# A two-block network on one Trainium2 core: where the norms between two layers are issued, and a tile order that goes k by k

## The chip, the cores and the metric

One Trainium2 chip, one of its cores. The metric is the time of the whole program on the device in microseconds (us), as the median of a few runs. Every time below is from these runs or from one execution that the hardware profiler recorded.

## What is computed

Two blocks of two layers each work on 512 tokens (T) of width 1024 (D). A layer is a mixer (block 1: sparse attention and an mLSTM; block 2: sparse and stick-breaking attention) and a feed-forward part (ffn). Around every one of these eight parts stands the same frame:

```python
h = rms_norm(x, pre_gain) * scale + shift      # what the part reads
y = part(h)                                    # ends in a product with an output matrix
x = x + gate * rms_norm(y, post_gain)          # what the next frame reads
```

rms_norm divides a token's 1024 values by the root of their mean square. So between the last product of one part and the first product of the next there lie two norms over the whole width, one behind the other. There are eight such ends: seven boundaries between parts, and the end of the program.

## The kernel before

**Layout.** Activations stand with the width on the 128 partitions: eight tiles (KT = 8) of 128 x 512 for x, for y and for h. All large products are made of 128x128 weight blocks. fp32 accuracy comes from three fast products: a weight chunk and h are each split into a high and a low part, and `mm3` (lines 310 to 315) issues high x high, high x low and low x high, one behind the other, so a weight chunk of 1024 columns times 256 tokens is 8 x 3 = 24 matmuls.

**Weights.** `load` (line 257) brings a chunk by DMA from the SP queue into a `raw` buffer (RAW = 4), rounds it on ScalarE into `hi` (line 265) and subtracts on VectorE, or on GpSimd where `lo_eng` says so, into `lo` (line 267). There are HL = 4 buffers for `hi` and 4 for `lo`; one is free again when the last matmul that reads it is done. Block 1's mixer converts `lo` on GpSimd; the other parts use VectorE.

**Halves.** At a boundary the work is done in two halves of 256 tokens (HALVES). `out_proj` (line 493, end of a mixer) and `down2` (line 1074, end of an ffn) run their last NO = 7 or ND = 5 output tiles in `in_halves` (line 340): all of them on half 0, then in reverse order on half 1. While half 1 is multiplied, half 0 is finished: `post_norm` of half 0 (line 475) is issued at the start of half 1, `pre_norm` of half 0 (line 437) before the tile number LA = 2 (out_proj, 24 matmuls a tile) or LB = 1 (down2, 33 matmuls a tile) of half 1. Behind the last tile `end()` issues `post_norm` of half 1.

**What a norm is.** `post_norm` makes two matmuls with a matrix of ones (ssy, sql; each is two records in the trace), Ln and Exp on ScalarE (rstd), and for each of the eight tiles two operations on VectorE (yn line 488, x line 489). `pre_norm` squares the eight x on ScalarE (line 444), adds them in pairs on VectorE (line 446), makes four matmuls with ones (eight records), again Ln and Exp, and for each tile xn on VectorE (line 458), hh on ScalarE (line 460 or 462) and hl on VectorE (line 468 or 473); hl follows three tiles behind xn (LAG = 3).

**The first products of the next part.** `fm_split` (line 376) takes them: six chunks of an ffn (EARLY = 6), three of block 1's mixer, four of block 2's. It too runs `in_halves`: tile by tile on half 0, then in reverse on half 1. `norms` leaves `pre_norm` of half 1 in `self.pending`; `fm_split` issues it before tile LC = 4 of half 0 (ffn), or before tile LD = 2 (mixers). In a mixer four steps of a product with tokens on the partitions (`more`, 24 matmuls a step; steps 0 and 1 read half 0, steps 2 and 3 half 1) come at the start of half 1. KF = 3 or KM = 1 weight chunks are kept for half 1.

**Around it.** At the start of a mixer `spill` (line 519) writes the eight x to DRAM with eight DMAs from the SP queue. Ahead of layer 1's ffn in block 1, `rope_tables` (line 544) computes sine and cosine tables for block 2; it is called between `out_proj` and `ffn`. The program's order is a priority and not the order itself: a scheduler fills each engine's queue when the program is built, by its own estimate of when an operand is ready, so a ready matmul may be put ahead of an earlier one that is not. Once built, each engine takes its queue in order.

Of the kernel before, what the change touches and what calls it, by code (L numbers as in the profile page):

```python
# [18 lines left out]
P = 128  # L19
T = 512  # L20
D = 1024
KT = D // P
# [10 lines left out]
PS1 = 0  # L33
PS2 = 0
# [9 lines left out]
PH2 = 0  # L44
PXM = 0
SA = 0
LA = 2
LAG = 3
LOA = 40
NO = 7  # L50
LB = 1
LC = 4
LD = 2
WIN = 0
KF = 3
KM = 1
# [20 lines left out]
HALVES = (slice(0, 256), slice(256, 512))  # L77
# [31 lines left out]
def steps(it, n):  # L109
    for _ in range(n):  # L110
        next(it, None)
        yield


def seq(*parts):
    for p in parts:
        yield from p
# [5 lines left out]
def dbg(g):  # L123
    while g.gi_yieldfrom is not None and hasattr(g.gi_yieldfrom, "gi_code") and g.gi_code.co_name in ("seq",):
        g = g.gi_yieldfrom
    l = g.gi_frame.f_locals if g.gi_frame else {}
    NET[0].mark(g.gi_code.co_name + "".join(str(l[v]) for v in ("g", "t", "bi", "pr", "hd") if v in l and isinstance(l[v], int)))


def run(steps):  # L130

    while True:
        try:
            dbg(steps)
            next(steps)
        except StopIteration as e:
            return e.value
# [16 lines left out]
class Task:  # L154
# [3 lines left out]
    def __init__(self, gen, n, start, end, after=None):  # L158
        self.gen, self.n, self.start, self.end, self.after = gen, n, start, end, after or {}
        self.i, self.done = 0, False  # L160
# [26 lines left out]
class Net:  # L187
    def __init__(self, ctx, tc, A, out):
        self.ctx, self.tc, self.nc, self.A, self.out = ctx, tc, tc.nc, A, out
        self.uid = 0  # L190
        self.fence = None
        self.back = iter(())
        NET[:] = [self]
        self.ahead = 90
        self.lo_eng = None
        self.T1, self.T2 = T1, T2
        self.pe = []
        self.xd = None
        self.pending = lambda: None
        self.tables, self.users = None, []  # L200
        nc = self.nc
        pool = lambda name, **kw: ctx.enter_context(tc.tile_pool(name=name, bufs=1, **kw))
        self.cp = pool("const")
        self.wp = pool("weights")
        self.up = ctx.enter_context(tc.tile_pool(name="units", bufs=1, reuse_waits="tile"))
        self.sp = pool("small")
        self.pp = pool("psum", space=PSUM)
        self.dp = pool("dram", space=DRAM)

        self.ident = self.cp.tile([P, P], F32, name="ident")  # L210
        make_identity(nc, self.ident)
        self.ones = self.cp.tile([P, P], F32, name="ones")
        nc.vector.memset(self.ones, 1.0)
        self.ones_r = self.cp.tile([P, P], F32R, name="ones_r")
        nc.scalar.activation(self.ones_r, self.ones, AF.Copy)
        self.eps = self.cp.tile([P, 1], F32, name="eps")
        nc.vector.memset(self.eps, EPS)


        self.cmask = self.cp.tile([P, T], F32, name="cmask")  # L220
        nc.gpsimd.memset(self.cmask, 0.0)
        nc.gpsimd.affine_select(self.cmask[:, 384:], self.cmask[:, 384:], [[-1, P]], ALU.is_ge, -NEG,
                                base=0, channel_multiplier=1)

        self.tri = self.cp.tile([P, P], F32, name="tri")
        nc.gpsimd.memset(self.tri, 0.0)
        nc.gpsimd.affine_select(self.tri, self.tri, [[-1, P]], ALU.is_ge, NEG, base=0, channel_multiplier=1)
        self.x = [self.unit("x") for _ in range(KT)]
        for k in range(KT):
            nc.sync.dma_start(self.x[k], A["xT"][:, k, :])  # L230
# [131 lines left out]
    def norms(self, y, sqs, g, nxt, late):  # L362


        if nxt is None:
            steps = [lambda i=i: self.post_norm(HALVES[i], y, sqs, g, True) for i in range(2)]
            return {0: steps[0]}, steps[1], (None, None)
        h = self.new_h()
        post = [lambda i=i: self.post_norm(HALVES[i], y, sqs, g) for i in range(2)]
        pre = [lambda i=i: self.pre_norm(HALVES[i], *nxt, *h) for i in range(2)]  # L370
        self.pending = pre[1]
        if late == 0:
            return {0: lambda: (post[0](), pre[0]())}, post[1], h
        return {0: post[0], late: pre[0]}, post[1], h

    def fm_split(self, chunks, act, pool, more=None):

        tiles = [self.ps("pj" if i < PJ else "ps") for i, _ in enumerate(chunks)]  # L380

        begin = {LC if more is None else LD: self.pending}
        middle = {} if more is None else {0: lambda: run(steps(more, 4))}
        self.in_halves([(i, [src]) for i, src in enumerate(chunks)], KF if more is None else KM,
                       lambda i, ws, hs, _: self.fm(tiles[i], ws[0], 0, act, hs, range(KT)), pool,
                       begin, middle)
        return tiles

    def fm_fed(self, chunks, toks, n, act, feed):
# [103 lines left out]
    def out_proj(self, chunks, act, y, g, nxt, pool):  # L493
# [19 lines left out]
        self.unspill()  # L513
        middle, end, h = self.norms(y, (ss, last), g, nxt, LA)
        self.in_halves([(f, [src for _, src in chunks(f)]) for f in range(KT - ntail, KT)], KO, one, pool, {}, middle)
# [164 lines left out]
    def mix1(self, l, h, nxt, feed=None):  # L680
        nc, A, tc = self.nc, self.A, self.tc
        par = self.par[l]
        W = A["w1_in"][l]
        act = self.acc(*h)
        pc = lambda name, i=0: par[:, B1[name] + i:B1[name] + i + 1]
        self.lo_eng = nc.gpsimd if LO1 else None
        self.spill()
        self.mark("1.split")


# [9 lines left out]
        def ev_vm(i, t, ps):  # L700
            nc.scalar.activation(vm[t][:, i * 256:i * 256 + 256], ps, AF.Copy)

        def ev_va(i, t, ps):
# [4 lines left out]
                              lambda t, ps, i=i: ev_vm(i, t, ps[:, :256])) for i in range(2)]  # L708
        if feed is None:
            more = seq(*vms)  # L710
            pss = self.fm_split([W[0], W[1], W[2]], act, PS1, more)
            run(more)
        else:
            pss, tps = self.fm_fed([W[0], W[1], W[2]], [(range(4), W[23]), (range(4, 8), W[24])], 256, act, feed)
            for t in range(NB):
                ev_vm(0, t, tps[t])
            self.rope_tables(A["positions"])
            run(vms[1])
# [201 lines left out]
        more = [Task(self.modulation(0, (2, 3, 4)), 24, *w("md"))] if l == 0 else []  # L920
# [153 lines left out]
    def down2(self, chunks, act, y, g, nxt, pool):  # L1074
# [16 lines left out]
        self.use(LN_EXP)  # L1091
        middle, end, h = self.norms(lambda k, cs: y[k][:, cs], (ss, last), g, nxt, LB)
        self.in_halves([(f, [src for _, src in chunks(f)]) for f in range(KT - ntail, KT)], KD, one, pool, {}, middle)
# [55 lines left out]
    def mix2(self, l, h, nxt):  # L1149
        nc, A, tc = self.nc, self.A, self.tc  # L1150
        par = self.par2[l]
        W = A["w2_in"][l]
        act = self.acc(*h)
        pc = lambda name, i=0, n=1: par[:, B2[name] + i:B2[name] + i + n]
        self.spill()
        self.mark("2.split")
        if LO2: self.lo_eng = nc.gpsimd

        vsb = self.values_tiles()
        sb_values = self.values_steps(vsb, [(W[16 + 2 * i], W[17 + 2 * i]) for i in range(2)], act)  # L1160
        pss = self.fm_split([W[i] for i in range(4)], act, PS2, sb_values)
        a1, a2 = self.rope(pss[0], pss[1])
        c1, c2 = self.rope(pss[2], pss[3], 64)

# [172 lines left out]
        for i, it in enumerate(items):  # L1337
            g, t, bi = it
            n = (2, 4, 8, 8)[t]
# [396 lines left out]
```

## Time and profile before

| | |
|---|---|
| median of 3 runs | 3232.23 us (3228.86 to 3241.45) |
| the profiled execution | 3238.15 us, span 3236.2 us, mean granted TensorE clock 0.975 |
| TensorE matmul (PE) busy | 3060.6 us, 95% of the span, 16196 instructions |
| VectorE (DVE), ScalarE (ACT), GpSimd (POOL) busy | 1958.9, 1552.1, 338.4 us |
| chain that ended last | PE 69%, DVE 10%, issue 10%, ACT 5%, DMA 3%, POOL 2% |

The profile page gives, for each engine, the time in which it had an instruction running, the wait ahead of an instruction and what ended it, and the clock that TensorE was granted (1.00 is 2.4 GHz, 0.50 is 1.2 GHz). A matmul's recorded duration is longer than its distance to the next, since they are pipelined; so the pace is read from starts, or from the number of matmuls in a stretch.

### The profile page before, as it was taken

Reading aid. Unit: us, or ns where it says so; the run is one execution under the profiler, and the core shown is the slowest. Engines: PE = TensorE matmul, PEld = TensorE weight load, DVE = VectorE, ACT = ScalarE, POOL = GpSimd, SP = SyncE. Lnnn points to the kernel's source line nnn. Section 1 sums busy time; section 2 is a strip of 40 time slices with the busy share of each in tenths; the row PEclk is TensorE's granted clock in tenths of the full one; section 3 lists DMA queues with packets and bytes.
Section 4 is the critical chain, followed back from the end, with each engine's and each line's share of the span. In section 5 each row is a group of like instructions: output and inputs, shape, how many; then the busy total and the mean of one; then the engine's idle time right before and its main releaser. Section 6 shows DMA issues by size and latency. Waiting matters only on the chain.

```text
span 3236.2 us, 42643 instructions
## 1 busy us (share of the span) xinstructions
PE 3060.6 (95%) x16196; PEld 2552.1 (79%) x16196; DVE 1958.9 (61%) x3542; ACT 1552.1 (48%) x2768; POOL 338.4 (10%) x329
## 2 busy tenths in 40 slices
PE   6898899998999899999999998999989999999998
PEld 5674787887875688888988778888888878788887
DVE  6778575546477463235677676645566766676365
ACT  4445642234444652224477665534445866454343
POOL 4352000001442000000100111000002001200000
PEclk8899999998998999999999999999999999999999
DMA  7235365644322232323421123323243112332323
GB/s 229 82 109 197 99 215 188 214 130 149 102 89 78 72 114 83 112 86 112 150 76 40 57 68 133 115 91 104 85 158 115 40 46 72 111 118 84 112 86 107
DMA packets 118925, 358.40 MB, mean 111 GB/s; under 512 B 15408, under 2 KB 28464, under 8 KB 118720
## 3 DMA queue, kind: packets, MB, share of 16 engines
q1 hardware_dynamic: 118720, 355.68, 34.2%
q8 instruction: 127, 2.08, 0.3%
q14 instruction: 78, 0.64, 0.1%
HBM read 336.19 MB, written 8.42 MB: 106 GB/s over the span
## 4 chain that ended last, share of the span: by engine, by line
PE 69%; DVE 10%; issue 10%; ACT 5%; DMA 3%; POOL 2%; SPq 0%; POOLq 0%; DVEq 0%; ACTq 0%
PE ps L305 26%; PE op L305 12%; PE pj L305 11%; PE dn L305 7%; PE tk L305 4%; PE nrm L305 2%; PE po L305 2%; DMA wm<-in_w_mod_dram 2%; DVE wlo L267 1%; DVE yn L488 1%; PE pt L308 1%; DVE x L489 1%; POOL mg L1357 1%; ACT whi L265 1%; DVE wm L633 1%
## 5 line engine op out<-in xcount | busy, mean ns | idle before, releaser
L265 ACT ACTIVATE whi<-raw 128x1024 fp32r<-128x1024 f32 (+1 forms) x562 | 550.0, 980 | 812.1 <-PE ps L305 204.0
L267 DVE TENSOR_TENSOR wlo<-raw,whi 128x1024 fp32r<-128x1024 f32 x500 | 559.1, 1122 | 530.5 <-ACT whi L265 527.4
L305 PE MATMUL ps<-hh,whi 128*128 128x512 f32 (+1 forms) x1560 | 574.4, 368 | 0.0
L305 PE MATMUL ps<-hl,whi 128*128 128x512 f32 (+1 forms) x1560 | 572.9, 367 | 0.0
L305 PE MATMUL ps<-hh,wlo 128*128 128x512 f32 (+1 forms) x1560 | 572.7, 367 | 0.0
L305 PE MATMUL pj<-hh,whi 128*128 128x512 f32 (+1 forms) x944 | 357.0, 379 | 23.5 <-ACT hh L654 13.3
L305 PE MATMUL pj<-hl,whi 128*128 128x512 f32 (+1 forms) x944 | 354.2, 375 | 4.4 <-POOL hl L656 4.4
L305 PE MATMUL pj<-hh,wlo 128*128 128x512 f32 (+1 forms) x944 | 352.1, 373 | 0.0
L305 PEld LDWEIGHTS ps<-hh,whi 128*128 128x128 f32 x1560 | 295.4, 189 | 48.1
L305 PEld LDWEIGHTS ps<-hh,wlo 128*128 128x128 f32 x1560 | 295.2, 189 | 48.3
L305 PEld LDWEIGHTS ps<-hl,whi 128*128 128x128 f32 x1560 | 295.5, 189 | 47.9
L305 PEld LDWEIGHTS pj<-hh,whi 128*128 128x128 f32 x944 | 181.5, 193 | 65.9 <-ACT hh L654 15.7
L305 PEld LDWEIGHTS pj<-hl,whi 128*128 128x128 f32 x944 | 181.9, 193 | 35.4 <-POOL hl L656 6.6
L305 PEld LDWEIGHTS pj<-hh,wlo 128*128 128x128 f32 x944 | 181.6, 192 | 30.2 <-issue 1.0
L633 DVE CUSTOM_DVE_ANT_0 wm<-wm,cact 128x1024 f32<-128x1024 f32 x96 | 121.6, 1270 | 112.1 <-DMA wm<-in_w_mod_dram 110.2
L267 POOL TENSOR_TENSOR wlo<-raw,whi 128x1024 fp32r<-128x1024 f32 x62 | 153.5, 2491 | 285.3 <-ACT whi L265 180.2
L305 PE MATMUL op<-hidh,whi 128*128 128x256 f32 (+1 forms) x572 | 178.9, 313 | 0.0
L305 PE MATMUL op<-hidh,wlo 128*128 128x256 f32 (+1 forms) x572 | 177.4, 310 | 0.3 <-DVE wlo L267 0.3
L305 PE MATMUL op<-hidl,whi 128*128 128x256 f32 (+1 forms) x572 | 176.9, 309 | 0.0
L575 POOL TENSOR_TENSOR rp<-rp,rp 128x512 f32<-128x512 f32 (+1 forms) x20 | 28.7, 1437 | 1091.7 <-DVE rp L574 1002.5
L305 PE MATMUL dn<-hidh,whi 128*128 128x512 f32 x352 | 137.8, 391 | 2.3 <-ACT hidh L254 2.3
L305 PE MATMUL dn<-hidl,whi 128*128 128x512 f32 x352 | 137.6, 391 | 0.2 <-DVE hidl L255 0.2
(352 smaller groups left out, 6151.4 us busy)
## 6 DMA issues: line engine op xcount, KB each, us to landing
raw<-in_w_in_dram SPq DMA_DIRECT2D x134, 512.0 KB, 3.4
raw<-in_w_up_dram SPq DMA_DIRECT2D x100, 512.0 KB, 3.5
wm<-in_w_mod_dram SPq DMA_DIRECT2D x96, 512.0 KB, 4.4
raw<-in_w_gu_dram SPq DMA_DIRECT2D x94, 512.0 KB, 3.4
raw<-in_w_dn_dram SPq DMA_DIRECT2D x80, 512.0 KB, 3.5
raw<-in_w_out_dram SPq DMA_DIRECT2D x52, 512.0 KB, 3.5
raw<-in_w_dn_dram SPq DMA_DIRECT2D x80, 192.0 KB, 3.1
hp<-rp SPq DMA_DIRECT2D x96, 64.0 KB, 2.0
```

Source lines behind the costliest of these rows:

```text
L265: nc_.scalar.activation(hi[:, :n], raw[:, :n], AF.Copy)
L267: (self.lo_eng or nc_.vector).tensor_tensor(lo[:, :n], raw[:, :n], hi[:, :n].bitcast(F32), ALU.subtract)
L305: return self.paced(self.nc.tensor.matmul(*args, **kw))
L308: return self.paced(self.nc.tensor.transpose(*args))
L488: nc.vector.scalar_tensor_tensor(t, y(k, hs), g[:, k:k + 1], r, ALU.mult, ALU.mult)
L489: (nc.gpsimd if PXM >> k & 1 else nc.vector).tensor_tensor(self.x[k][:, hs], self.x[k][:, hs], t, ALU.add)
L575: nc.gpsimd.tensor_tensor(t1[r], t1[r], t2[r], ALU.subtract)
L633: self.nc.vector.tensor_tensor_reduce(raw, raw, self.cact, 1.0, 0.0, ALU.mult, ALU.add, self.mod[l][:, c:c + 1])
L1357: nc.gpsimd.tensor_tensor(s, s, gate[1, f], ALU.add)
```

## The change

Three things are changed, at the seven boundaries alone (the end of the program keeps its order).

1. `pre_norm` of half 0 is issued later: before tile LA = 4 instead of 2 in `out_proj`, before tile LB = 3 instead of 1 in `down2`.
2. `post_norm` of half 1 is no longer issued at the end of `out_proj` or `down2` but inside `fm_split`, behind its first eight `mm3` (24 matmuls). `pre_norm` of half 1 comes behind 40 `mm3` (LC = 5) in an ffn; in a mixer it comes behind the whole of half 0 and two steps of `more`. The other two steps come behind half 1. `spill` moves with `post_norm` of half 1, from the start of the mixer to just behind it.
3. `fm_split` goes through groups of up to four tiles (KG = 4): within a group all tiles take k = 0, then all take k = 1, and so on, where before a tile took all eight k. In an ffn the groups are four and two tiles, in a mixer one group of three or four.

```diff
-LA = 2
+LA = 4
-LB = 1
-LC = 4
-LD = 2
+LB = 3
+LC = 5
+KG = 4
...
-        self.pending = pre[1]
-        if late == 0:
-            return {0: lambda: (post[0](), pre[0]())}, post[1], h
-        return {0: post[0], late: pre[0]}, post[1], h
+        self.pending = post[1], pre[1]
+        return {0: post[0], late: pre[0]}, lambda: None, h
 
-    def fm_split(self, chunks, act, pool, more=None):
+    def fm_split(self, chunks, act, pool, more=None, spill=False):
         tiles = [self.ps("pj" if i < PJ else "ps") for i, _ in enumerate(chunks)]
-        begin = {LC if more is None else LD: self.pending}
-        middle = {} if more is None else {0: lambda: run(steps(more, 4))}
-        self.in_halves([(i, [src]) for i, src in enumerate(chunks)], KF if more is None else KM,
-                       lambda i, ws, hs, _: self.fm(tiles[i], ws[0], 0, act, hs, range(KT)), pool,
-                       begin, middle)
+        n, keep = len(chunks), KF if more is None else KM
+        late = None if more is not None else LC * KT
+        kept, loads, count = {}, 0, 0
+        ah, al = act
+        for hs in HALVES:
+            first = hs is HALVES[0]
+            if not first and more is not None:
+                run(steps(more, 2))
+                self.pending[1]()
+            order = list(range(n)) if first else list(range(n))[::-1]
+            for o in range(0, n, KG):
+                group = []
+                for i in order[o:o + KG]:
+                    ws = kept.pop(i, None)
+                    if ws is None:
...
+                        ws = self.load(chunks[i])
...
+                    if first and i >= n - keep:
+                        kept[i] = ws
+                    group.append((i, ws))
+                for k in range(KT):
+                    c = slice(k * P, k * P + P)
+                    for i, (hi, lo) in group:
+                        if count == KT:
+                            self.pending[0]()
+                            if spill:
+                                self.spill()
+                        if count == late:
+                            self.pending[1]()
+                        count += 1
+                        self.mm3(tiles[i][:, hs], hi[:, c], lo[:, c], ah(k, hs), al(k, hs), k == 0, k == KT - 1)
+        if more is not None:
+            run(steps(more, 2))
         return tiles
```

In `mix1` and `mix2` the call `self.spill()` at the start is taken out and `fm_split` is called with `spill=True`; layer 0 of block 1, whose first products are made in `fm_fed` (line 389), keeps its call.

## Rows read from the trace of the kernel before

**Rows 1.** The profile page: its first part and the chain that ended last.
```profile
PE 3060.6 (95%) x16196; PEld 2552.1 (79%) x16196; DVE 1958.9 (61%) x3542; ACT 1552.1 (48%) x2768; POOL 338.4 (10%) x329
...
PE 69%; DVE 10%; issue 10%; ACT 5%; DMA 3%; POOL 2%; SPq 0%; POOLq 0%; DVEq 0%; ACTq 0%
```

**Rows 2.** Busy time by stretch: stretch, length, engines (count), PEclk, DMA share, GB/s.
```profile
356.11:374.94 18.83, 18.83 (x159) 18.83 (x157) 9.64 (x12) 10.58 (x20) 0.00 (x0) 1.00 0.51 168
```

**Rows 3.** The same view: the third of the seven boundaries, and the sum of all.
```profile
1119.68:1196.44 76.76, 65.86 (x483) 63.11 (x481) 55.37 (x110) 40.77 (x76) 0.00 (x0) 0.91 0.31 100
...
sum 527.70, PE 471.89 PEld 456.63 DVE 371.42 ACT 268.91 POOL 40.93; mean PE 67.41 PEld 65.23 DVE 53.06 ACT 38.42 POOL 5.85
```

**Rows 4.** The same view: stretches around half 0's pre_norm matmuls, sum of seven.
```profile
381.77:388.86 7.09, 3.35 (x10) 2.56 (x9) 5.99 (x13) 4.32 (x12) 0.00 (x0) 0.76 0.26 88
759.39:769.12 9.73, 3.95 (x11) 3.04 (x10) 7.44 (x19) 3.45 (x11) 0.00 (x0) 0.75 0.26 74
...
sum 58.53, PE 26.04 PEld 19.42 DVE 46.27 ACT 27.61 POOL 0.00; mean PE 3.72 PEld 2.77 DVE 6.61 ACT 3.94 POOL 0.00
```

**Rows 5.** The same view: stretches around half 1's norm matmuls, with their sum.
```profile
1162.04:1173.23 11.19, 4.04 (x12) 2.84 (x10) 9.37 (x21) 4.68 (x10) 0.00 (x0) 0.72 0.33 116
1543.54:1552.34 8.80, 5.66 (x19) 4.75 (x18) 6.53 (x14) 3.51 (x9) 0.00 (x0) 0.64 0.84 287
2394.16:2398.24 4.08, 0.94 (x6) 0.70 (x5) 4.08 (x11) 3.51 (x9) 0.00 (x0) 1.00 1.01 387
sum 38.86, PE 15.54 PEld 12.14 DVE 31.29 ACT 17.50 POOL 8.96; mean PE 3.11 PEld 2.43 DVE 6.26 ACT 3.50 POOL 1.79
```

**Rows 6.** Timeline, PE: start, us, instruction, [idle before]. The first boundary.
```profile
374.94 0.59 PE L305 MATMUL nrm<-ssy,ones 128*128 128x256 f32 x2
...
385.68 0.80 PE L305 MATMUL nrm<-sq,ones 128*128 128x256 f32 x1 [3.74 <-DVE sq L446]
...
403.91 0.28 PE L305 MATMUL pj<-hl,whi 128*128 128x256 f32 x1
404.03 0.59 PE L305 MATMUL nrm<-ssy,ones 128*128 128x256 f32 x2
...
416.06 1.89 PE L305 MATMUL nrm<-sq,ones 128*128 128x256 f32 x8
417.60 0.47 PE L305 MATMUL ps<-hh,whi 128*128 128x256 f32 x1
```

**Rows 7.** Timeline, DVE: the last pair of squares at the first boundary.
```profile
387.34 0.42 DVE L446 TENSOR_TENSOR sq<-sq,sq 128x256 f32<-128x256 f32 x1
```

**Rows 8.** Timeline, ACT and DVE: one weight chunk's conversion in steady running.
```profile
2036.14 1.06 ACT L265 ACTIVATE whi<-raw 128x1024 fp32r<-128x1024 f32 x1 [1.82 <-PE ps L305]
...
2037.23 1.23 DVE L267 TENSOR_TENSOR wlo<-raw,whi 128x1024 fp32r<-128x1024 f32 x1 [1.66 <-ACT whi L265]
```

**Rows 9.** Timeline, PE, ACT and DVE: behind half 1's pre_norm at the sixth boundary.
```profile
2400.06 0.47 PE L305 MATMUL ps<-hh,wlo 128*128 128x256 f32 x1
...
2400.45 0.47 ACT L275 ACTIVATE rstd<-nrm,eps 128x256 f32<-128x256 f32 x1 [2.70 <-PE nrm L305]
...
2401.92 0.81 ACT L460 ACTIVATE hh<-xn 128x256 fp32r<-128x256 f32 x2 [0.55 <-DVE xn L458]
...
2403.00 0.42 DVE L468 TENSOR_TENSOR hl<-xn,hh 128x256 fp32r<-128x256 f32 x1
```

**Rows 10.** Timeline, ACT: the third boundary, where the rope tables are made.
```profile
1167.67 0.63 ACT L275 ACTIVATE sin<-r 128x512 f32<-128x512 f32 x1 [7.06 <-DVE r L564]
1168.20 2.23 ACT L444 ACTIVATE sq<-x 128x256 f32<-128x256 f32 x7
```

**Rows 11.** Timeline, POOL and DVE: the second boundary, weights converted on GpSimd.
```profile
781.95 9.90 POOL L267 TENSOR_TENSOR wlo<-raw,whi 128x1024 fp32r<-128x1024 f32 x4 [104.94 <-PE op L305]
...
784.89 4.75 DVE L1087 TENSOR_TENSOR ssy<-ssy,sqy 128x256 f32<-128x256 f32 x2
```

**Rows 12.** Busy time by stretch: fm_fed, which goes k by k over its tiles.
```profile
72.00:78.00 6.00, 6.00 (x52) 6.00 (x51) 0.27 (x1) 0.77 (x2) 4.36 (x2) 1.00 0.79 236
```

More of the change, by code (lines that the diff above doesn't have):

```diff
@@ L198, in __init__ @@
         self.xd = None
-        self.pending = lambda: None
+        self.pending = None
         self.tables, self.users = None, []
@@ new lines, in norms @@
+        return {0: post[0], late: pre[0]}, lambda: None, h
+    def fm_split(self, chunks, act, pool, more=None, spill=False):
+        tiles = [self.ps("pj" if i < PJ else "ps") for i, _ in enumerate(chunks)]
+        n, keep = len(chunks), KF if more is None else KM
[13 more added lines that the diff above has]
+                    if ws is None:
+                        old = self.lo_eng
+                        if pool >> loads & 1:
+                            self.lo_eng = self.nc.gpsimd
+                        loads += 1
+                        ws = self.load(chunks[i])
+                        self.lo_eng = old
+                    if first and i >= n - keep:
[14 more added lines that the diff above has]
+            run(steps(more, 2))
@@ L686, in mix1 @@
         self.lo_eng = nc.gpsimd if LO1 else None
-        self.spill()
         self.mark("1.split")
@@ L710, in mix1 @@
             more = seq(*vms)
-            pss = self.fm_split([W[0], W[1], W[2]], act, PS1, more)
+            pss = self.fm_split([W[0], W[1], W[2]], act, PS1, more, spill=True)
             run(more)
         else:
+            self.spill()
             pss, tps = self.fm_fed([W[0], W[1], W[2]], [(range(4), W[23]), (range(4, 8), W[24])], 256, act, feed)
@@ L1154, in mix2 @@
         pc = lambda name, i=0, n=1: par[:, B2[name] + i:B2[name] + i + n]
-        self.spill()
         self.mark("2.split")
@@ L1160, in mix2 @@
         sb_values = self.values_steps(vsb, [(W[16 + 2 * i], W[17 + 2 * i]) for i in range(2)], act)
-        pss = self.fm_split([W[i] for i in range(4)], act, PS2, sb_values)
+        pss = self.fm_split([W[i] for i in range(4)], act, PS2, sb_values, spill=True)
         a1, a2 = self.rope(pss[0], pss[1])
```

## The prediction, made before the changed kernel was run

> **What bounds the kernel now.** I read the page first: PE is busy 95% of the span and has 69% of the chain that ended last [rows 1]. So nothing that VectorE or ScalarE does counts unless PE waits for it, and a gain can only be time in which PE stands still or runs at half clock. Then I went by stretch through the seven boundaries, from the first matmul of half 0's post_norm to the last 256-token product of fm_split. In an undisturbed stretch 157 products take 18.83 us, 0.12 us each [rows 2]; eight norm records take 1.54 us, 0.19 each [rows 6]. The seven stretches last 527.70 us [rows 3]. By the code they hold 3543 matmul records: 480 in each of the four ahead of an ffn, 525 and twice 549 in those ahead of a mixer; 168 are norm records. At pace that is 3375 x 0.12 + 168 x 0.19 = 437 us. So 91 us are lost at the seven boundaries, 2.8% of the span, and this is the most that the change can give.
>
> Where do they lie? In two kinds of stretch. Ahead of half 0's pre_norm PE waits for the squares: post_norm starts at 374.94, the first pair is ready at 385.68 after 3.74 us of waiting [rows 6], and the clock in the stretch is 0.76, 0.75 at the second boundary [rows 4]. These seven stretches last 58.53 us [rows 4]; their norm records take 7 x 1.54 = 10.8 and some six products 0.7, so 47 us are lost. Around half 1's norms five stretches last 38.86 us [rows 5]; their work (four pre_norms, one post_norm pair, some 13 products) is 8 us, so 31 are lost. The other 13 us are the ends of half-clock stretches and small waits.
>
> **Part 1, half 0's pre_norm later: most of the 47 us goes.** From post_norm's first matmul to the last pair of squares the chain takes 387.76 - 374.94 = 12.8 us [rows 6, 7]. Afterwards four tiles of 24 products stand in between in out_proj, 96 x 0.12 + 0.6 = 12.1 us, and three tiles of 33 in down2, 12.5 us. So PE arrives within a us of the squares. In the time won, one or two more tiles are converted on VectorE (1.23 us each [rows 8]), which can stand ahead of the squares. I leave 0.5 us a boundary, 3.5 in all (0 to 14). What is late next: h of half 0 has 72 or 66 products less one norm as cover, about 8 us, and needs about 3.4 us for its first tile [rows 9]; k by k it is then asked for one tile in 1.4 us. No wait.
>
> **Part 2 and 3, half 1's norms and the groups.** That half 1's post_norm is 24 products later costs PE nothing by itself: its squares come about 12.8 us after it and 96 products (11.5 us) or, in a mixer, 112 to 136 (13 to 16 us) lie in between. What takes the place of the 31 us:
>
> - *Ends of groups.* Each chunk needs one of four hi and lo buffers (HL = 4), and a group of four holds all four until its last k. A freed chunk is followed by 1.06 us on ACT, then 1.23 on DVE [rows 8]. The first tile's last matmul lies nine products, 1.1 us, ahead of the group's end. For its release I take 0.25 us, an estimate: a product's record lasts 0.28, 0.16 beyond the pace [rows 6], and an engine wakes some hundredths later. So the next hi is ready 0.3 us behind the end, its lo 1.5, the second lo 2.8. PE waits about 1.5 us (1 to 2.4) unless something else is ready. Behind the first group this comes seven times, 10.5 us (7 to 17). Behind the second half's group it comes four times in an ffn, 6 us, and three times in a mixer, where two steps of more can cover it, 1.5 us: 7.5 (3 to 14).
> - *Starts of fm_split.* All four chunks are wanted within 1.1 us, while the fourth buffer is freed by the last product of out_proj or down2. 0 where the scheduler puts ready products of the first three tiles ahead, 1.5 where it doesn't; 0.75 for six boundaries, 4.5. At the second boundary GpSimd converts at 2.5 us a chunk (four in 9.90) [rows 11]: 2. In all 6.5 (0 to 13).
> - *Start of half 1.* At the sixth boundary the next product follows the norm's last matmul at 2400.06; hh of the first tile is ready 2.3 us later, hl 3.4 [rows 9]. In the mixers nothing lies in between any more, so PE waits about 3.3 us, three times, 9.9. A wait of this size has cost a fallen clock at the fourth boundary (0.64 in the stretch) and none at the sixth (1.00) [rows 5], so I add 3 in all (0 to 10). In an ffn 24 products (2.9 us) lie in between: 0.85 x 4 = 3.4. Sum 16.3 (13 to 24).
> - *Third boundary.* rope_tables puts a sine on ACT that waits 7.06 us for VectorE, with seven of the eight squares behind it [rows 10]; that is most of the 11.19 us there [rows 5]. After the change post_norm of half 1 comes behind rope_tables too, and its Ln and Exp need another activation table than the sine, so it can't pass. pre_norm is 2 us later, but its chain starts behind the tables: I keep 9.5 of 9.6 us (5 to 13).
> - *Second boundary.* While GpSimd converts four chunks in 9.90 us, two additions on VectorE take 4.75 us in place of about 0.75 [rows 11]. So each conversion held one up by about 2 us; one to four of them now meet post_norm's 16 operations: 5 us (2 to 8) stay.
> - *spill* adds nothing: eight DMAs that waited for x before wait for it now; behind them on SP stand weight loads that raw buffers hold back anyway (0, at most 2 a mixer).
>
> Sum: 3.5 + 10.5 + 7.5 + 6.5 + 16.3 + 9.5 + 5 = 59 us stay lost or are new, against 91. Gain 32 us. By the low ends (0, 7, 3, 0, 13, 5, 2) 30 stay and the gain is 61; by the high ends (14, 17, 14, 13, 24, 13, 8, and 6 for the DMAs) it is -18. The profiled execution took 3238.15 us, its span 3236.2; the median is 5.9 lower. 3238.15 - 32 = 3206, and by the median 3200.
>
> **A rule against the change.** fm_fed already goes k by k over up to seven PSUM tiles; in such a stretch 51 products take 6.00 us at clock 1.00, 0.12 each [rows 12], the pace of [rows 2]. So I charge nothing for the order itself. The Trainium skill (TensorE: Matmul & The Clock Gate, "A second HAM failure mode: psum-queue depth-cycling") tells of a kernel that cycled through PSUM banks, let the engine idle in bits between groups, and lost throughput as the clock fell and rose again. By that rule the grouped products would run at half clock. The row here does not bear it out.
>
> **Rivals.**
> (A) The forecast, 3200, its own range 3184 to 3216. Chance 0.50.
> (B) The scheduler fills the holes. For it: it put products of the next part ahead of a norm matmul that was not ready (the pj product at 403.91 belongs behind the norm at 404.03 by the program [rows 6]). Against: at a group's end nothing else may be ready. Then the ends of groups and the starts cost almost nothing, 24.5 us less lost: 3176. Chance 0.20.
> (C) The wait moves. Half 0's gain is real, but half 1's norms now end on the critical path: each start of half 1 waits 3.3 us or more, with a fallen clock each time, and the groups' ends take the upper bounds. For it: the 3.4 us of [rows 9] and the clocks of [rows 5]. Against: in an ffn there are products in between. 85 of 91 us stay: 3226. Chance 0.18.
> (D) Slower: the four weight buffers. If each group's chunks are converted only behind the group before, and two or three of them are needed before PE can go on, each group's end costs 1.06 + 2 x 1.23 + 0.25 = 3.8 us and a fallen clock of about 2.4 (0.25 of 9.73 us, [rows 4]): 6.2 us at 14 ends, 87, beside 3.5 + 16.3 + 9.5 + 5 = 34. 121 against 91: 30 us slower, 3262. It decides from about 4 us an end upwards. Against: a tile is released every 0.36 us at a group's end, and k by k the other tiles go on. Chance 0.08.
> (E) The rule on cycling, as a mechanism of this kernel: 4 x 288 + 144 + 2 x 192 = 1680 grouped products at 0.24 us in place of 0.12 are 202 us more: 3402. Chance 0.02.
> The last 0.02 are for changes of order elsewhere, of either sign.
>
> **How the numbers follow.** The likeliest is (A), 3200. The range must leave out at most 0.2: from (B)'s middle less 6 us to above (C), 3170 to 3232; it leaves out (D), (E) and the low part of (B). A measurement of this kernel can tell about 0.5%, 16 us, from no change. Faster by more than that (below 3216): most of (A), 0.45, (B) 0.20, a little of (C): 0.67. Within: 0.05 of (A), 0.16 of (C), 0.02 of the rest: 0.23. Slower: (D), (E): 0.10.
>
> **What the profile after would show.** Right: no wait for sq at half 0's pre_norm in all seven places, clock 1.00 there; waits for whi and wlo of 1 to 2 us at groups' ends; a wait for hh or hl of about 3 us at the start of half 1 in the three mixers; the sine still ahead of half 1's squares at the third boundary. Wrong: PE still waits for squares at half 0 (conversions stand ahead of them on VectorE); no waits at groups' ends (then B); waits above 4 us with a clock of 0.5 behind each (then C or D); pace above 0.12 within a group (then E).

## The result, and the profile after

The kernel after takes 3251.93 us (median of 6 runs, 3247.66 to 3259.53), the kernel before 3233.18 us beside it (6 runs, 3228.86 to 3241.45). The ratio is 1.0057, 95% interval 1.0039 to 1.0075: the change costs 19 us where 32 were to be gained. The profiled execution of after took 3252.04 us, its span is 3250.1, 13.9 more than before.

The page of after: busy time of TensorE (PE) and the other engines, and the chain that ended last.

```profile
PE 3070.9 (94%) x16196; PEld 2556.3 (79%) x16196; DVE 1960.1 (60%) x3542; ACT 1551.9 (48%) x2768; POOL 335.8 (10%) x329
...
PE 69%; issue 10%; DVE 9%; ACT 4%; DMA 2%; POOL 2%; POOLq 0%; SPq 0%; DVEq 0%; ACTq 0%
```

As many instructions as in [rows 1], and the same bound. So the answer lies where the forecast looked, in the seven boundaries. Busy time by stretch, columns as in [rows 2]; the third boundary, and the sum of all seven:

```profile
1116.75:1199.57 82.82, 68.20 (x482) 64.72 (x481) 54.03 (x109) 39.97 (x76) 0.00 (x0) 0.88 0.24 81
...
sum 543.94, PE 482.51 PEld 459.40 DVE 368.45 ACT 265.16 POOL 38.55; mean PE 68.93 PEld 65.63 DVE 52.64 ACT 37.88 POOL 5.51
```

The third was 76.76 and the sum 527.70 in [rows 3]; read up to the next product of 512 tokens, as here, the sum of before is 528.40. The stretches grew by 15.5 us; the span grew by less, since other parts got 1.6 us shorter.

Half 0's pre_norm at the first boundary after: PE, ScalarE (ACT) and VectorE (DVE), start, us, instruction, [idle before and what ended it].

```profile
387.33 0.28 PE L305 MATMUL op<-ch,wlo 128*128 128x256 f32 x1
390.57 1.13 PE L305 MATMUL nrm<-sq,ones 128*128 128x256 f32 x4 [2.96 <-DVE sq L476]
...
387.53 1.06 ACT L265 ACTIVATE whi<-raw 128x1024 fp32r<-128x1024 f32 x1 [1.27 <-PE op L305]
388.49 0.37 ACT L534 ACTIVATE y<-op 128x256 f32<-128x256 f32 x1
388.75 0.38 ACT L536 ACTIVATE sqy<-op 128x256 f32<-128x256 f32 x1
389.02 2.55 ACT L474 ACTIVATE sq<-x 128x256 f32<-128x256 f32 x8
...
382.64 0.75 DVE L519 TENSOR_TENSOR x<-x,yn 128x256 f32<-128x256 f32 x2
383.32 0.41 DVE L538 TENSOR_TENSOR ssy<-ssy,sqy 128x256 f32<-128x256 f32 x1
...
390.09 1.32 DVE L476 TENSOR_TENSOR sq<-sq,sq 128x256 f32<-128x256 f32 x3
```

The wait of 3.74 us in [rows 6] is still there, as 2.96 us, although four tiles stand ahead of the norm and the last x is done at 383.4. The squares start at 389.02 all the same: they stand in ScalarE's queue behind the conversion and the evictions (y, sqy) of the tiles that the call was moved past, and those wait for PE.

**A table for all that follows.** In each kernel's trace I cut the seven stretches at the norms and took from each piece its matmuls at pace (0.12 us a product, 0.19 a norm record, [rows 2, 6]); the rest is time lost, waits and half clock together. The pieces: *half 0*, from post_norm's first matmul to the last of half 0's pre_norm; *to the end*, the rest of out_proj or down2; *fm_split*, up to half 1's pre_norm; *norm 1*, the wait for half 1's pre_norm, its matmuls, and the wait for h right behind them; *behind*, the rest. Early squares 0 or 1 means that the squares of that half are issued right behind its post_norm. Times are medians; before, measured again beside the experiments, took 3233.4 to 3235.2. The pieces are read from one profiled execution of each kernel; two rows with the same program order, after and UNITS = 69, differ by 1.2 us in all and by up to 0.9 in a piece.

| kernel | time, us | half 0 | to the end | fm_split | norm 1 | behind | lost |
|---|---|---|---|---|---|---|---|
| before | 3233.2 | 46.4 | 10.7 | 4.8 | 26.3 | 2.9 | 91.1 |
| after (parts 1, 2, 3) | 3251.9 | 33.3 | 3.9 | 25.0 | 27.9 | 16.6 | 106.7 |
| part 1 alone | 3240.3 | 32.0 | 3.9 | 12.3 | 39.3 | 4.4 | 91.9 |
| part 2 alone | 3233.1 | 46.0 | 5.1 | 2.2 | 23.9 | 10.6 | 87.8 |
| parts 1, 2 | 3228.5 | 32.6 | 2.4 | 10.1 | 28.0 | 11.9 | 85.0 |
| parts 2, 3 | 3257.6 | 47.3 | 6.9 | 18.7 | 22.3 | 17.4 | 112.6 |
| after, groups of two | 3238.5 | 32.8 | 2.8 | 15.9 | 29.4 | 10.6 | 91.4 |
| after, UNITS = 69 | 3251.8 | 32.4 | 3.3 | 25.5 | 27.3 | 16.9 | 105.5 |
| same, five weight buffers | 3229.8 | 29.7 | 1.7 | 10.8 | 28.6 | 12.2 | 82.9 |
| after, early squares 0 | 3216.1 | 4.0 | 1.2 | 25.0 | 27.6 | 15.7 | 73.6 |
| part 1, early squares 0 | 3206.6 | 4.0 | 1.2 | 13.6 | 39.5 | 5.3 | 63.5 |
| before, early squares 0 | 3227.5 | 35.9 | 8.3 | 5.1 | 28.7 | 3.4 | 81.3 |
| parts 1, 2, early squares 0 | 3194.7 | 4.0 | 1.2 | 12.1 | 27.4 | 10.3 | 55.1 |
| parts 1, 2, early squares 0, 1 | 3192.5 | 4.0 | 1.2 | 11.1 | 20.9 | 8.4 | 45.7 |
| before, rope tables later | 3221.0 | 46.1 | 10.1 | 3.9 | 17.2 | 2.2 | 79.5 |
| all that helped | 3172.8 | 4.0 | 1.2 | 10.6 | 5.5 | 7.4 | 28.8 |

### The profile page after: what moved, and what is told of

Its sections match the earlier page's. It is cut to its first block, busy times and chain, and to the rows that moved or that the text cites. A ratio compares the mean times of both kernels' runs of the same rounds, so it can differ in the third digit from the quotient of the medians.

```text
span 3250.1 us, 42634 instructions
## 1 busy us (share of the span) xinstructions
PE 3070.9 (94%) x16196; PEld 2556.3 (79%) x16196; DVE 1960.1 (60%) x3542; ACT 1551.9 (48%) x2768; POOL 335.8 (10%) x329
## 4 chain that ended last, share of the span: by engine, by line
PE 69%; issue 10%; DVE 9%; ACT 4%; DMA 2%; POOL 2%; POOLq 0%; SPq 0%; DVEq 0%; ACTq 0%
PE ps L305 27%; PE op L305 12%; PE pj L305 11%; PE dn L305 7%; PE tk L305 4%; PE po L305 2%; PE nrm L305 2%; DVE wlo L267 1%; PE pt L308 1%; DMA wm<-in_w_mod_dram 1%; DVE yn L518 1%; DVE ss L1509 1%; POOL mg L1386 1%; ACT whi L265 1%; DVE x L519 1%
## 5 line engine op out<-in xcount | busy, mean ns | idle before, releaser
L305 PE MATMUL tk<-wlo,hh 128*128 128x256 f32 (+1 forms) x448 | 130.2, 291 | 9.5 <-DVE wlo L267 5.0
```

Source lines behind the costliest of these rows:

```text
L305: return self.paced(self.nc.tensor.matmul(*args, **kw))
```

## The experiments

My theory after the result was S: the squares on ScalarE and the pair sums on VectorE move with the call of pre_norm, so the wait moves with it. The rivals: the groups cost it (G), or half 1's norms, issued later, do.

### One part alone, or one part less

```diff
-LA = 2
+LA = 4
-LB = 1
+LB = 3
```

> Part 1 alone: the kernel before with LA = 4 and LB = 3, all else as it was. Theory S (the squares on ScalarE and the pair sums on VectorE are issued by pre_norm and move with it, behind the conversions and evictions of the tiles ahead of the call): PE still waits about 3 us for half 0's squares in all seven places, in place of 3.9 and 5.9 us, so the gain is 1 to 3 us a boundary: 3212 to 3228. The forecast's theory (the squares are done 12.8 us after post_norm began, wherever the call stands): the wait is gone, 40 us less, about 3193.

3240.25 us, ratio to before 1.0018 (1.0007 to 1.0029): outside both ranges. S was right at half 0, where PE still waits in all seven places (46.4 to 32.0 us lost) and 6.8 more went behind it. But those 21 us came back: norm 1 went from 26.3 to 39.3 and fm_split from 4.8 to 12.3. The fourth boundary of this kernel, ScalarE, VectorE, then PE:

```profile
1534.28 0.42 ACT L460 ACTIVATE hh<-xn 128x256 fp32r<-128x256 f32 x1 [1.45 <-DVE xn L458]
1534.61 0.40 ACT L1085 ACTIVATE sqy<-y 128x256 f32<-128x256 f32 x1
...
1534.17 1.42 DVE L468 TENSOR_TENSOR hl<-xn,hh 128x256 fp32r<-128x256 f32 x4
1535.52 0.41 DVE L1087 TENSOR_TENSOR ssy<-ssy,sqy 128x256 f32<-128x256 f32 x1
...
1536.18 0.59 PE L305 MATMUL nrm<-ssy,ones 128*128 128x256 f32 x2
1536.61 0.59 PE L305 MATMUL nrm<-sql,ones 128*128 128x256 f32 x2
1544.74 2.60 PE L305 MATMUL nrm<-sq,ones 128*128 128x256 f32 x5 [6.36 <-DVE sq L446]
```

The last sum that half 1's post_norm needs (ssy) is late on two engines: its operand sqy, whose own input is done at 1526.46, stands on ScalarE behind half 0's last hh, and ssy itself stands on VectorE behind half 0's last four hl. In before ssy comes 0.4 us ahead of the last product of down2, here 5.8 us behind it. PE uses that time for products of fm_split: by count of the trace's records 38 of the 48 that the program puts between the two norms of half 1 run ahead of post_norm and 10 behind it, where in before all 48 ran behind. So the cover of the second norm is spent: 6.36 us of waiting, where before waited 3.1.

The other way round, the kernel after with LA = 2 and LB = 1:

> Parts 2 and 3 alone: the kernel after with LA = 2 and LB = 1 put back. Theory S: the waits at half 0 are again 3.9 and 5.9 us, so 1 to 3 us a boundary more than after: 3257 to 3272. Rival L (part 1 itself does the harm, and parts 2 and 3 pay): below the kernel before, 3205 to 3230. By the sizes of the forecast (44 us of 91 stay in these parts, 47 at half 0 unchanged): 3233 + 3 to 10.

3257.56 us, 1.0070 (1.0055 to 1.0085), as S expected. Beside the other two parts, part 1 gives 5.6 us between the medians, with intervals that overlap, and 5.9 us of lost time. Parts 2 and 3 together cost 23 us against before.

Part 3 left out of after:

```diff
-KG = 4
+KG = 1
```

> Parts 1 and 2 without part 3: the kernel after with KG = 1, so the first tiles go tile by tile again and half 1's norms stay late. Rival G (the groups are what costs: all four weight buffers held until a group's end, 1.4 us at each first group and 1.9 us at each second): 14 ends of 1.4 to 1.9 us are gone, 3225 to 3235. Theory N (the late norms of half 1 cost it: PE waits for h at the start of half 1): no change against the kernel after, 3245 to 3255.

3228.45 us, 0.9983 (0.9974 to 0.9992): the groups are worth 23.5 us of loss, all that after loses and 5 us more. Parts 1 and 2 together gain a little. Against part 1 alone, part 2 takes norm 1 from 39.3 to 28.0.

Part 2 alone (KG = 1, LA = 2 and LB = 1 in the kernel after):

> Part 2 alone: the kernel after with KG = 1, LA = 2, LB = 1 (half 1's norms late, half 0's pre_norm and the order tile by tile as before). If the parts add: part 3 cost 24 us in the presence of part 1, so 3257.6 - 24 = 3234; part 1 gave 5.6 us with part 2 present (3257.6 to 3252), so part 2 alone is 3234, about no change against before, and its 12 us gain beside part 1 is only the undoing of what part 1 pushed into half 1's norms. If part 2 pays by itself: 3218 to 3228.

3233.08 us, 0.9997 (0.9988 to 1.0007): no change, as the first branch expected. Part 3 adds: it costs 24.5 us beside part 2 and 23.5 beside parts 1 and 2. Parts 1 and 2 do not add: alone they change the time by +5.5 us and by nothing clear, together by -6. Part 2 pays 12 us beside part 1, because it puts 96 to 120 products between half 1's norms in the mixers in place of 48, of which part 1 had used up most (behind half 1's post_norm the records show 85 and 97 with both parts, 10 to 13 with part 1 alone). Without part 1 it pays nothing. The moved spill was not run by itself; it comes with part 2, so no cost of it shows.

### Squares that do not move

Half 0's squares and pair sums right behind half 0's post_norm; matmuls, xn, hh and hl stay where the change put them. `squares` holds the eight squares and four pair sums; the last two lines stand at the end of `post_norm`:

```diff
-    def pre_norm(self, hs, gs, sh, hh, hl):
-
+    def squares(self, hs):
...
+        return res
+
+    def pre_norm(self, hs, gs, sh, hh, hl):
...
+        sqs = self.sums.pop(hs.start, None) or self.squares(hs)
+        ps = self.ps("nrm")
+        for i, s2 in enumerate(sqs):
+            self.matmul(ps[:, :256], self.ones, s2, start=i == 0, stop=i == len(sqs) - 1)
...
+        if not end and hs.start in (0,):
+            self.sums[hs.start] = self.squares(hs)
```

> The kernel after, but half 0's squares and pair sums are issued right behind half 0's post_norm, where the kernel before has the matmuls that read them too; the matmuls and the rest of pre_norm stay where the change put them. Theory S: no wait for sq at half 0's pre_norm in all seven places (3.1 us before it at four, 3.7 at three, plus half-clock stretches): 20 to 35 us less than after, 3217 to 3232. Rival V (ScalarE then stands waiting for x with evictions and conversions behind it, and PE waits for weights or PSUM tiles instead): 3245 to 3260.

3216.07 us, 0.9943 (0.9929 to 0.9958), 36 us less than after, 1 us below the range of theory S. The first boundary, ACT and PE; then the sum of the seven stretches:

```profile
384.20 2.56 ACT L473 ACTIVATE sq<-x 128x256 f32<-128x256 f32 x8
386.66 0.36 ACT L545 ACTIVATE sqy<-op 128x256 f32<-128x256 f32 x1
386.92 0.37 ACT L543 ACTIVATE y<-op 128x256 f32<-128x256 f32 x1
...
388.80 0.28 PE L306 MATMUL op<-ch,wlo 128*128 128x256 f32 x1
388.91 1.89 PE L306 MATMUL nrm<-sq,ones 128*128 128x256 f32 x8
```

```profile
sum 510.86, PE 469.21 PEld 448.79 DVE 367.77 ACT 263.57 POOL 39.12; mean PE 67.03 PEld 64.11 DVE 52.54 ACT 37.65 POOL 5.59
```

The squares start 7.9 us behind post_norm's start in place of 14.2, and now the evictions wait for them; the norm follows the product ahead of it at pace. Lost at half 0: 4.0 us in all. The delayed evictions cost nothing that the table shows (to the end: 1.2). Rival V falls.

Without the groups:

> Parts 1 and 2 without the groups (KG = 1), and half 0's squares and pair sums issued right behind half 0's post_norm. If the two effects add (squares early: 36 us less, measured on the kernel after; groups left out: 24 us less, measured on the kernel after), 3252 - 36 - 24 = 3192, range 3185 to 3202. If they overlap (the wait that is taken away at half 0 comes back at half 1, as it did with part 1 alone), 3205 to 3216.

3194.65 us, 0.9885 (0.9869 to 0.9901): the two effects add.

Two runs split what was open about part 1. Part 1 alone with early squares of half 0:

> Part 1 alone (LA = 4, LB = 3 on the kernel before), now with half 0's squares and pair sums issued right behind half 0's post_norm, so that they do not move with pre_norm. Open: the 13 us that part 1 alone added at half 1's norms. If they too came from half 0's late squares (all of half 0's chain late on ScalarE and VectorE), both go: 3240 - 28 - 13 = 3199, range 3193 to 3207. If they come from the later pre_norm itself, whose conversions meet half 1's post_norm whatever the squares do: only half 0's 28 us go, 3208 to 3216.

3206.63 us, 0.9912 (0.9896 to 0.9927), 34 us less than part 1 alone. The time lies at the upper end of the first range and 1.4 us under the second; the table decides for the second: half 0's loss falls by 28.0, norm 1 stays at 39.5. (The execution profiled took 3214.79 us, the longest of five from 3201.76 on.) In its trace ssy again comes 5.8 us behind the last product at the sixth boundary, and the same wait of 6.36 us follows. So the wait at half 1 is not from the late squares but from half 0's later xn, hh and hl.

And before with early squares and pre_norm where it was:

> The kernel before with half 0's squares and pair sums right behind half 0's post_norm and pre_norm where it was (LA = 2, LB = 1). The first pair is then ready about 9.6 us behind post_norm's start in place of 10.3 in out_proj and 8.7 in place of 10.5 in down2, PE is at the norm after 6 us. If a cover of products is needed besides the early squares: the waits shrink by 0.7 to 1.8 us only, 3218 to 3229. If the squares' place is all that matters: as with part 1 and early squares, 3195 to 3210.

3227.50 us, 0.9971 (0.9959 to 0.9984): the waits shrink by 0.7 to 1.8 us each. Early squares without the later call give 6 us, the later call without early squares costs 5, both together gain 27.

### What the groups cost

> The kernel after with groups of two tiles (KG = 2) in place of four. Rival G1 (the cost of the groups is that all four pairs of weight buffers are held until a group's last k, so the next chunk is converted too late): two pairs stay free for the next group, most of the 24 us goes, 3228 to 3236. Rival G2 (the cost lies in the order k by k itself, whatever the size): half or more of it stays, 3240 to 3252.

3238.49 us, 1.0018 (1.0005 to 1.0031), between the two ranges: 13 of 23.5 us go. That alone does not tell buffers from order. The next two do: groups of four, with five pairs of weight buffers against four, at the same UNITS (the number of activation buffers, lowered to make room).

```diff
-HL = 4
-UNITS = 73
+HL = 5
+UNITS = 69
```

> The kernel after with five pairs of converted weight buffers in place of four (HL = 5, UNITS = 69 to make room). Rival G1 (a group of four holds all four pairs until its last k, so the next chunk is converted too late): against its control with UNITS = 69 and four pairs it is 6 to 15 us faster, the waits for whi and wlo at the ends of the first groups fall, while second chunks still wait. Rival G2 (the buffers don't matter): within 4 us of the control.

> Control for the run with five pairs: the kernel after with UNITS = 69 and four pairs of weight buffers. It shows what four units less cost alone: 3248 to 3265 by either theory.

3229.80 us (0.9981, 0.9972 to 0.9990) against 3251.80 (1.0047, 1.0034 to 1.0060): 22 us, more than I expected of one pair. Lost in fm_split 10.8 in place of 25.5, behind 12.2 in place of 16.9, which is what leaving out the groups gives (10.1 and 11.9). PE's waits at the sixth boundary (engine, line, what it waited for: us, times, longest), four pairs, then five:

```profile
PE nrm L305 <- DVE sq L476: 4.3, 2, 2.8
PE tk L305 <- DVE wlo L267: 2.5, 1, 2.5
PE ps L305 <- ACT hh L490: 2.0, 1, 2.0
PE op L305 <- DVE wlo L267: 0.6, 1, 0.6
```

```profile
PE nrm L305 <- DVE sq L476: 3.7, 2, 2.1
PE ps L305 <- ACT hh L490: 2.0, 1, 2.0
```

Here every wait for a converted weight is gone; over all seven stretches such waits of PE fall from 19.2 to 0.9 us. The four pairs held to a group's last k are the cost of the groups; with a fifth, groups are as good as single tiles (3229.8 and 3228.5), and no better. Single tiles with five pairs were not run.

### Half 1's squares, the rope tables, and all together

Half 1's squares early too (hs.start in (0, 256) in the diff above):

> As the kernel with parts 1 and 2 and early squares of half 0, but half 1's squares and pair sums too are issued right behind half 1's post_norm. In the mixers PE waited 1.70 us for half 1's squares, behind the evictions of the token product; if that is the squares' place in ScalarE's queue again, three mixers gain 1.7 to 4 us each: 5 to 12 us less than without. In the ffns no such wait was seen, so no change there; the third boundary's wait stays (rope_tables stands ahead). If the squares' place is not what holds them: within 3 us.

3192.50 us, 0.9872 (0.9853 to 0.9890). By the medians, 2 us less than without, this is the branch "within 3 us", and a gain in time is not shown. In the stretches the squares' place is what holds them: PE's wait for half 1's squares, 1.54 us in each of the three mixers (the expectation had 1.70), becomes 0.3, 0 and 0, and the seven stretches are 9.4 us shorter, the three in the mixers by 10.0. In the profiled executions 9 us came on elsewhere (last section).

The rope tables made inside the ffn, on the kernel before:

```diff
+                if l == 1 and f == 3:
+                    self.rope_tables(A["positions_2"])
                 return t
...
-            if l == 1:
-                self.rope_tables(A["positions_2"])
             gu, dn = A["w1_gu"][l], A["w1_dn"][l]
```

> The kernel before, with rope_tables for block 2 called inside the ffn's first up part (behind the fourth gate's SiLU) instead of between out_proj and ffn. Theory R (the sine on ScalarE holds half 1's squares at the third boundary): the 7.3 us wait falls to under 1 us as at the other three ffn boundaries, whose stretch is 66 us in place of 77, so 8 to 11 us less: 3222 to 3227. Rival (VectorE's and ScalarE's load at that place is the cause, or the tables hold something up inside the ffn): 3230 to 3236.

3220.97 us, 0.9965 (0.9947 to 0.9983), 12 us less than before beside it, 1 us below the range of theory R. The third boundary, waits of PE before (first line) and with the tables later (second), and that stretch, 67.12 us in place of 76.76 [rows 3]. The wait that is left is half 0's:

```profile
PE nrm L305 <- DVE sq L446: 10.9, 2, 7.1
```

```profile
PE nrm L305 <- DVE sq L446: 3.8, 1, 3.8
```

```profile
1114.30:1181.42 67.12, 63.37 (x482) 61.65 (x481) 47.56 (x93) 36.83 (x72) 0.00 (x0) 0.95 0.33 111
```

All together, with half 1's pre_norm in the mixers one step of more earlier:

```diff
-                run(steps(more, 2))
+                run(steps(more, 1))
                 self.pending[1]()
+                run(steps(more, 1))
```

> All that helped so far together: parts 1 and 2 without groups (KG = 1), squares of both halves right behind their post_norm, rope_tables inside the ffn, and in the mixers half 1's pre_norm one token step earlier (one step of more ahead of it, one behind), so that 24 products cover h of half 1's first tile. Additive: 3192.5 for the first three, 12 us less for rope_tables, 4 to 6 us less for the 2.2 us wait at the start of half 1 in three mixers: 3172 to 3182. If the waits move again: 3182 to 3192.

3172.79 us, 0.9804 (0.9791 to 0.9818): 62 us less than before, 79 less than after. The sixth boundary's waits, three stretches and the sum of seven:

```profile
PE pj L306 <- DVE hl L506: 0.5, 1, 0.5
PE op L306 <- DVE wlo L268: 0.3, 1, 0.3
```

```profile
747.76:828.02 80.26, 70.80 (x528) 68.04 (x526) 55.29 (x97) 42.80 (x80) 27.03 (x12) 0.94 0.42 141
1099.18:1159.68 60.50, 60.50 (x483) 59.38 (x481) 47.45 (x93) 36.72 (x72) 0.00 (x0) 1.00 0.38 122
...
2304.24:2375.14 70.90, 69.93 (x552) 67.64 (x551) 57.77 (x115) 39.65 (x75) 5.76 (x6) 1.00 0.52 168
sum 466.02, PE 452.67 PEld 440.89 DVE 362.97 ACT 265.33 POOL 38.54; mean PE 64.67 PEld 62.98 DVE 51.85 ACT 37.90 POOL 5.51
```

Six boundaries run at clock 1.00; 28.8 us stay lost, 15.5 of them at the second boundary, where GpSimd converts the weights (clock 0.94).

## Why the prediction was wrong, step by step

The bound and the place were right: 91 us lost before, as the forecast had it, and nearly all of the change's effect inside the seven stretches. The forecast left 59 us there; 106.7 are left. The 47.9 us between lie in these steps.

- **Part 1, half 0 (3.5 forecast, 33.3 measured): the step that failed.** It said that from post_norm to the last pair of squares "the chain takes 387.76 - 374.94 = 12.8 us", and took that as fixed, wherever the call stands. But the eight squares and four sums are pre_norm's own instructions and move with it. In before they ran right behind the x only because the call stood there; 0.5 us a boundary was left for conversions that "can stand ahead of the squares", where in fact every eviction of the tiles passed stands ahead on ScalarE, and each of these waits for PE itself. So the squares move along with the tiles that were to cover them: of 46 us, 13 went. That the cover was sized rightly is seen where the squares stay: 4.0 us lost in place of 3.5. The forecast's own sign of being wrong, PE still waiting for squares at half 0, is what the trace showed, on ScalarE behind evictions in place of on VectorE behind conversions.
- **What is late next behind part 1.** "No wait" was written for half 0's h; none worth a line was seen in the ffns, but at the second boundary PE waits 4.2 us for half 0's hl with parts 1 and 2. More harm was one step further, and not in the sum. With part 1 alone, half 0's conversions meet half 1's last sums on ScalarE and VectorE, at the fourth and sixth boundary post_norm of half 1 comes 6.5 us behind the last product instead of at once, and PE spends the products that were to cover its second norm. In after, part 2's products make up for that.
- **Half 1's norms (0 forecast in the mixers).** The forecast gave "112 to 136" products, 13 to 16 us, as cover and charged nothing. By the code it is 96 to 120, since the first eight mm3 are 24 products and not 8, and by the records of after 85 and 91. PE waits there in all three mixers, since the squares stand behind the evictions (vh) of the token product, at the fourth boundary until 1559.81 though the last x is done at 1551.1: the same error again. Of the 14.7 us that norm 1 loses in the mixers nearly 8 are this; the other 7 are the wait for hh right behind, which belongs to the next term. With half 1's squares early (and no groups) 7.7 are left, nearly all of it the wait for hh. The fourth boundary of after, PE and ACT:

```profile
1552.25 0.38 PE L305 MATMUL tk<-wlo,hh 128*128 128x256 f32 x1 [2.52 <-DVE wlo L267]
1561.04 2.53 PE L305 MATMUL nrm<-sq,ones 128*128 128x256 f32 x8 [1.54 <-DVE sq L476]
1565.54 0.50 PE L305 MATMUL ps<-hh,whi 128*128 128x256 f32 x2 [1.98 <-ACT hh L490]
...
1559.53 0.38 ACT L254 ACTIVATE vh<-tk 128x256 fp32r<-128x256 f32 x1 [2.39 <-PE tk L305]
1559.81 2.54 ACT L474 ACTIVATE sq<-x 128x256 f32<-128x256 f32 x8
```

- **Start of half 1** (16.3 forecast): the wait for hh is there, 1.98 us here in place of 3.3. In the mixers 6.9 us are lost by it, and all of *behind* without groups is 11.9, together 18.8. Under by 2.5.
- **Third boundary** (9.5): 13.2 us are lost at its half 1 norm. That the tables stand in the way was right, and moving them settles it; in after it is post_norm's own Ln that stands behind them. Its matmuls are at 1151.0, the Ln (rstd) at 1164.69:

```profile
1162.76 0.63 ACT L275 ACTIVATE cos<-r 128x512 f32<-128x512 f32 x1 [3.20 <-DVE r L594]
1163.40 1.28 ACT L288 ACT_TABLE_LOAD   x1
1164.69 0.47 ACT L275 ACTIVATE rstd<-nrm,eps 128x256 f32<-128x256 f32 x1
```

- **Second boundary** (5): fm_split there loses 7.8 us even without groups, 4.2 of it the waits for hl named above. Under by 6.5 together with the third.
- **Groups (10.5 + 7.5 + 6.5 = 24.5): right in the main.** Leaving them out gives back 21.7 us of lost time, 23.5 in the medians, and the five buffers show that the mechanism was the one named. By the terms, PE's waits for weights are 9.2 us at the first groups' ends, 4.2 at those of the second half, and 3.7 at the starts, all at the second boundary. The first group's end waits for hi, then lo, of the next chunk (first boundary of after):

```profile
414.66 0.38 PE L305 MATMUL ps<-hh,whi 128*128 128x256 f32 x1 [0.44 <-ACT whi L265]
...
415.79 0.39 PE L305 MATMUL ps<-hh,wlo 128*128 128x256 f32 x1 [0.62 <-DVE wlo L267]
```

So these terms make up the difference: half 0 by 29.8, behind it 3.9, half 1's norms and what follows by 19 (8 for the squares in the mixers, 2.5 for the start of half 1, 6.5 for the third and second boundary, 2 for the rest of fm_split), less 5 for the groups. Part 1 was the only gain in the sum, and parts 2 and 3 were costs throughout: with 46.4 us at half 0 less than a third gone, the costs outweigh it. Of the rivals, (C) named the right kind (the wait moves, half 1 ends on the path), with half 0's gain called real, of which only 13 us were, and a price of 3226; (D) named the right resource at 14 ends of 6.2 us, where all groups' ends and starts together cost 23.5 us in the medians; its size was 3262. (B) is out: PE waits at the groups' ends. (E) is out: within the first group of the last boundary the pace is [rows 2]'s,

```profile
2874.00:2880.00 6.00, 6.00 (x51) 5.97 (x51) 4.80 (x14) 1.65 (x4) 0.00 (x0) 1.00 0.10 39
```

51 records in 6.00 us, 0.12 each, at 1.00, the level of 2.4 GHz. The Trainium skill (TensorE: Matmul & The Clock Gate, "A second HAM failure mode: psum-queue depth-cycling") has the clock fall and rise where PSUM banks are cycled with short idle times between groups. This window has no idle time, so it shows only that cycling through four tiles cost no clock by itself there. Half clock lay in 61 us of the seven stretches in after and in 65 in before. With the fifth buffer, which takes the waits at the groups' ends away, it is 44 against 58 in its control: those idle times did go with a fallen clock, as that section has it, by 14 us and not for all grouped products.

## What to carry to other kernels

When a step is moved, list its instructions on every engine, and ask of each what it will now stand behind in that engine's queue: a wait is covered by later work only if its producers stay where they were. Split such a step, so that its producers are issued as soon as their inputs exist and only its consumer on the busy engine is late. Before tiles are interleaved, count the buffers that they hold together: with none left to prepare the next, the order cost 22 us here, and with one more pair it gained nothing over single tiles.

## What the runs showed of the hardware

The same instructions with nearly the same waits ran at either clock level, and whole runs of one kernel move with the granted clock: twelve runs with groups of two lie between 3228.94 us at a mean clock of 0.982 and 3249.41 at 0.975. Between the second and the third boundary the kernels with parts 1 and 2 and early squares, of half 0 or of both halves, have the same order of TensorE records; in each PE waited 1.1 us ahead of the same product, shortly behind another wait (1.5 us with both halves early, 1.4 with half 0 alone). From that product to the same later one, first both halves early, then half 0 alone:

```profile
996.44:1054.84 58.40, 56.07 (x178) 28.62 (x178) 27.20 (x80) 35.91 (x74) 7.74 (x14) 0.85 0.08 18
```

```profile
993.48:1045.28 51.80, 48.80 (x178) 25.77 (x178) 27.01 (x80) 35.78 (x74) 7.71 (x14) 1.00 0.08 21
```

178 records in both, 58.40 us at a clock of 0.85 and 51.80 at 1.00: 6.6 us that no wait of PE accounts for. The whole part between these boundaries took 269 us in three of the profiled kernels and 271 to 280 in the others, with 7 to 31 us of it at 1.2 GHz. What decides which level is granted there stays open; it is as large as several of the effects above, and it is why the table of lost time, and not the medians alone, was used to tell them apart.
